# First SwiGLU of a hybrid DiT layer: input products as seven products of quarters, output sums accumulated in DRAM

## The chip, the cores and the metric

The kernel runs on one core of a Trainium2 chip. Its engines, each with its own instruction stream in order, are TensorE (PE; PEld is its loading of weights), VectorE (DVE), ScalarE (ACT), GpSimd (POOL) and SyncE (SP), which here only starts DMAs. DMAs go through 16 shared engines. The metric is device time in microseconds (us) of one execution.

## The reference

One layer of a diffusion transformer, batch 1, 512 latent tokens x (width 1024) and 256 context tokens ctx. What matters here is its first part, a modulated SwiGLU of width 2816 on both streams:

```python
def modulate(x, w, shift, scale):
    return rmsnorm(x, w) * (1 + scale) + shift

def swiglu(x, w_in, w_out):
    a, b = jnp.split(x @ w_in, 2, axis=-1)
    return (jax.nn.silu(a) * b) @ w_out
...
        h = h + 0.5 * g1 * swiglu(modulate(h, norm_ffn1[layer], sh1, sc1), w_ffn1_in[layer], w_ffn1_out[layer])
        hc = hc + 0.5 * g1c * swiglu(modulate(hc, norm_ffn1[layer], sh1c, sc1c), w_ffn1_in[layer], w_ffn1_out[layer])

        u = modulate(h, norm_mix[layer], sh2, sc2)
        uc = modulate(hc, norm_mix[layer], sh2c, sc2c)
...
        h = h + g2 * mixer_output(o, rg, cv, ga, gb, *branch_w)

        h = h + 0.5 * g3 * swiglu(modulate(h, norm_ffn2[layer], sh3, sc3), w_ffn2_in[layer], w_ffn2_out[layer])
    return rmsnorm(h, final_norm)
```

The shifts, scales and gates are nine vectors for each stream, c @ w_mod (1024 x 9216). Between the two SwiGLUs stand the retention, the convolution and their merge; the context ends with its keys and values.

## The kernel before

Channels lie on the 128 partitions, tokens in the free dimension, so an activation is eight blocks of 128 channels (`h0`..`h7` with 512 latent tokens, `hc` with 256 context tokens). Every product is in three matmuls (`mm3`, L90 to L92): each operand is split into a high part in fp32r and the low rest, and high x high, low x high and high x low are added up in PSUM. A weight unit (512 KB: `wraw`, four buffers) is loaded by SP, cast by ACT to `wh` (L81) and its rest taken by DVE as `wl` (L83). PSUM has eight banks of 512 columns (`ps`).

The first SwiGLU has 22 chunks of 128 hidden channels, each with two column blocks of w_in (the two halves a and b), in three groups of 8, 7 and 7 (`GROUPS`). A chunk multiplies both blocks with all eight channel blocks of the normed latent tokens (`uh`, `ul`: 48 matmuls of 512 columns) and of the context tokens (`uc`: 48 of 256). Then ACT takes the silu and DVE multiplies (L297, L304) and takes the low parts (L279). After a group, four out units multiply the group's chunks with w_out, two channel blocks each, and DVE adds the result, times the gate, to `h` and `hc` in SBUF (`residual`, L427). In the last group, the last two units come apart: four context products first, then the latent tokens by halves of 256, while ACT and DVE already sum the squares and norm the result for the next part (`tail1`, L252 to L271), and POOL saves h to `hdram`.

The first two chunks are computed in `start`, as the norms of the eight channel blocks come; the modulation vectors that these need are computed there by PE, DVE (L161) and POOL (L164) from loads of w_mod (`first_mods`). The 56 other modulation products (`mods`: one or two VectorE instructions of 1024 elements, L184) are spread beside the first SwiGLU by `mod_step`, two after each chunk and out unit. A scheduler sets each engine's order from the program and the tiles' waits; tiles of one tag share buffers, `t` has six.

## Time and profile before

Median of three runs 1779.48 us (1778.73 to 1779.65). The profiled execution has a span of 1775.7 us; some 3.8 us lie around the span.

| what | value |
|---|---|
| span of the profiled execution | 1775.7 us |
| time, median of 3 runs | 1779.48 us |
| ACT casts of weights, L81 | 248, 1.04 us each |
| DVE low parts of weights, L83 | 248, 1.21 us each |
| DVE residuals of the first SwiGLU, L427 | 68, 44.6 us |
| bytes moved by DMA | 199.95 MB, mean 113 GB/s |

A row of a timeline is start, duration, engine, line, operation and tiles; a group of equal rows has its count (x4). A matmul's duration includes its way through the array, so the price of one in a row is the distance between two starts.

### The profile page before, as it was taken

Reading aid. Unit: us, or ns where it says so; the run is one execution under the profiler, and the core shown is the slowest. Engines: PE = TensorE matmul, PEld = TensorE weight load, DVE = VectorE, ACT = ScalarE, POOL = GpSimd, SP = SyncE. Lnnn points to the kernel's source line nnn. Section 1 sums busy time; section 2 is a strip of 40 time slices with the busy share of each in tenths; the row PEclk is TensorE's granted clock in tenths of the full one; section 3 lists DMA queues with packets and bytes.
Section 4 is the critical chain, followed back from the end, with each engine's and each line's share of the span. In section 5 each row is a group of like instructions: output and inputs, shape, how many; then the busy total and the mean of one; then the engine's idle time right before and its main releaser. Section 6 shows DMA issues by size and latency. Waiting matters only on the chain. (4 is left out here: it accounts for less than half of the span.)

```text
span 1775.7 us, 22456 instructions
## 1 busy us (share of the span) xinstructions
PE 1749.0 (98%) x9182; PEld 1498.7 (84%) x9182; DVE 1038.7 (58%) x1646; ACT 575.1 (32%) x809; POOL 65.9 (4%) x111
## 2 busy tenths in 40 slices
PE   6999999999999999999999999999999999999997
PEld 4788888888889988888888888888888988888887
DVE  7755825452444798793876679293755643333335
ACT  5422113211222532432342334233562432222222
POOL 4100000000000000000000000001100000000000
PEclk8999999999999999999999999999999999999999
DMA  9133523362433321152142125114652133233321
GB/s 349 37 119 119 187 74 121 127 194 74 133 121 125 103 92 64 60 166 71 49 144 94 60 72 173 65 48 166 201 196 102 60 119 95 97 95 97 103 84 48
DMA packets 60156, 199.95 MB, mean 113 GB/s; under 512 B 7250, under 2 KB 7250, under 8 KB 60052
## 3 DMA queue, kind: packets, MB, share of 16 engines
q1 hardware_dynamic: 53140, 176.20, 29.8%
q0 software_dynamic: 6336, 21.25, 3.6%
q8 instruction: 72, 1.18, 0.3%
q10 hardware_dynamic: 576, 1.05, 0.2%
q14 instruction: 32, 0.26, 0.0%
HBM read 185.89 MB, written 12.58 MB: 112 GB/s over the span
## 5 line engine op out<-in xcount | busy, mean ns | idle before, releaser
L81 ACT CAST wh<-wraw 128x1024 fp32r<-128x1024 f32 (+1 forms) x248 | 257.2, 1038 | 640.3 <-PE ps L91 390.1
L83 DVE TENSOR_TENSOR wl<-wraw,wh 128x1024 fp32r<-128x1024 f32 (+1 forms) x248 | 298.5, 1206 | 255.9 <-ACT wh L81 251.7
L92 PE MATMUL ps<-uh,wl 128*128 128x512 f32 (+1 forms) x992 | 373.5, 377 | 2.2 <-DVE wl L83 2.2
L90 PE MATMUL ps<-uh,wh 128*128 128x512 f32 (+1 forms) x992 | 375.4, 380 | 0.3 <-ACT uh L270 0.3
L91 PE MATMUL ps<-ul,wh 128*128 128x512 f32 (+1 forms) x992 | 373.5, 377 | 0.0
L90 PE MATMUL ps<-gx,wh 128*128 128x512 f32 (+1 forms) x748 | 277.6, 373 | 0.2 <-ACT gx L278 0.2
L92 PE MATMUL ps<-gx,wl 128*128 128x512 f32 (+1 forms) x748 | 277.6, 372 | 0.0
L91 PE MATMUL ps<-gx,wh 128*128 128x512 f32 (+1 forms) x748 | 277.5, 372 | 0.0
L92 PEld LDWEIGHTS ps<-uh,wl 128*128 128x128 f32 x992 | 187.2, 189 | 37.2 <-DVE wl L83 2.9
L90 PEld LDWEIGHTS ps<-uh,wh 128*128 128x128 f32 x992 | 186.9, 189 | 34.7 <-issue 1.1
L91 PEld LDWEIGHTS ps<-ul,wh 128*128 128x128 f32 x992 | 187.3, 189 | 33.4 <-issue 0.5
L515 DVE SCALAR_TENSOR_TENSOR h<-y,vec,h 128x512 f32<-128x512 f32 x240 | 179.7, 749 | 5.4
L90 PEld LDWEIGHTS ps<-gx,wh 128*128 128x128 f32 x748 | 140.7, 188 | 24.6 <-ACT gx L278 0.4
L92 PEld LDWEIGHTS ps<-gx,wl 128*128 128x128 f32 x748 | 140.5, 188 | 24.6
L91 PEld LDWEIGHTS ps<-gx,wh 128*128 128x128 f32 x748 | 140.6, 188 | 24.0
L91 PE MATMUL ps<-uc,wh 128*128 128x256 f32 (+1 forms) x508 | 150.9, 298 | 0.2 <-DVE uc L271 0.2
L90 PE MATMUL ps<-uc,wh 128*128 128x256 f32 (+1 forms) x508 | 150.6, 297 | 0.3 <-ACT uc L270 0.3
L92 PE MATMUL ps<-uc,wl 128*128 128x256 f32 (+1 forms) x508 | 150.5, 297 | 0.0
L427 DVE SCALAR_TENSOR_TENSOR h<-ps,g_x,h 128x512 f32<-128x512 f32 (+1 forms) x68 | 44.6, 656 | 129.5 <-PE ps L92 129.2
L91 PE MATMUL ps<-gc,wh 128*128 128x256 f32 (+1 forms) x320 | 102.6, 321 | 0.0
L90 PE MATMUL ps<-gc,wh 128*128 128x256 f32 (+1 forms) x320 | 102.4, 320 | 0.0
L92 PE MATMUL ps<-gc,wl 128*128 128x256 f32 (+1 forms) x320 | 102.4, 320 | 0.0
(217 smaller groups left out, 2195.7 us busy)
## 6 DMA issues: line engine op xcount, KB each, us to landing
wraw<-in_w_mod SPq DMA_DIRECT2D x56, 512.0 KB, 3.5
wraw<-in_w1i SPq DMA_DIRECT2D x44, 512.0 KB, 3.8
wraw<-in_w2i SPq DMA_DIRECT2D x44, 512.0 KB, 3.7
wraw<-in_w_cv SPq DMA_DIRECT2D x16, 512.0 KB, 3.7
wraw<-in_w_v SPq DMA_DIRECT2D x16, 512.0 KB, 6.5
wraw<-in_w_rg SPq DMA_DIRECT2D x16, 512.0 KB, 3.6
wraw<-in_w_ro SPq DMA_DIRECT2D x16, 512.0 KB, 3.8
ypart<-t POOLq DMA_DIRECT2D x32, 256.0 KB, 4.3
```

The costliest lines, as they stand in the source:

```text
L81: nc.scalar.copy(hi, raw)
L83: nc.vector.tensor_sub(lo, raw, f32(hi))
L90: nc.tensor.matmul(o, w[0], x[0], start=first, stop=False)
L91: nc.tensor.matmul(o, w[0], x[1], start=False, stop=False)
L92: nc.tensor.matmul(o, w[1], x[0], start=False, stop=last)
L427: nc.vector.scalar_tensor_tensor(dst, p, g[:, b:b + 1], dst, ALU.mult, ALU.add)
L515: nc.vector.scalar_tensor_tensor(o, y[:, t:t + L], vec[:, w0 + t:w0 + t + 1], o, ALU.mult, ALU.add)
```

## The change

Four chunks stay as they are. For the other 18, the two column blocks of w_in and the tokens are taken as quarters: the contraction of 1024 channels in two halves of 512, the output as block a and block b, and the 768 tokens (latent and context side by side, tiles `uh`/`ul` now of 768) as two halves of 384. Strassen's scheme, in Winograd's form, replaces the eight products of quarters by seven, each with four channel blocks and three matmuls: 84 matmuls of 384 columns instead of 96. The sums of the tokens' quarters are made once (`operands`), those of the weights for every chunk, and the results are added up by VectorE and in PSUM (`chunk`).

```diff
+GROUPS1 = ((0, 4), (4, 4), (8, 4), (12, 4), (16, 3), (19, 3))
+LA = L + LC
+H = LA // 2
...
+    def operands(kb):
+        b1, b2 = hx[kb], hx[kb + 4]
+        b11, b12, b21, b22 = b1[:, :H], b1[:, H:], b2[:, :H], b2[:, H:]
+        ta, tb = t_((P, 2, H), F32, "wy", 2), t_((P, 2, H), F32, "wy", 2)
+        nc.vector.tensor_sub(ta[:, 0, :], b11, b12)
+        nc.vector.tensor_sub(ta[:, 1, :], b12, b22)
+        nc.vector.tensor_sub(tb[:, 0, :], ta[:, 1, :], b11)
+        nc.vector.tensor_add(tb[:, 1, :], b21, tb[:, 0, :])
...
+            split(hi, lo, t)
...
+    def chunk(j, u, t):
...
+        w0 = weights(r0)
+        nc.vector.tensor_add(y0[:, 0, :], a21, a11)
+        nc.vector.tensor_add(y0[:, 1, :], a21, a22)
+        w1 = weights(y0.rearrange("p a b -> p (a b)"))
+        nc.vector.tensor_add(y1[:, 0, :], y0[:, 1, :], a11)
+        nc.vector.tensor_add(y1[:, 1, :], y1[:, 0, :], a12)
+        w2 = weights(y1.rearrange("p a b -> p (a b)"))
+        w3 = weights(a22)
...
+        product(pa, w0, 0, part(u[:4], lo_), True)
+        nc.scalar.copy(p1, pa)
+        product(pd, w1, 0, [x[1] for x in t], True)
+        nc.scalar.copy(p7, pd)
+        product(pa, w0, 1, part(u[4:], lo_), False)
+        nc.scalar.activation(s[:, lo_], pa, AF.Silu)
+        product(pc, w1, 1, [x[0] for x in t], True)
+        nc.vector.tensor_sub(p7, p7, pc)
+        product(pb, w2, 0, [x[2] for x in t], True)
+        nc.vector.tensor_add(p1, p1, pb)
+        nc.vector.tensor_sub(c[:, hi_], p7, p1)
+        product(pc, w2, 1, part(u[4:], hi_), False)
+        nc.vector.tensor_add(s[:, hi_], p1, pc)
+        nc.scalar.activation(s[:, hi_], s[:, hi_], AF.Silu)
+        product(pd, w3, 0, [x[3] for x in t], False)
+        nc.vector.tensor_sub(c[:, lo_], pd, p1)
+        nc.vector.tensor_mul(s, s, c)
```

SBUF doesn't hold h beside the new operands. So h and hc live in DRAM during the first SwiGLU: two DRAM copies put x and ctx there at the start, each out unit of the first five groups sends its scaled result by accumulating DMAs, and the last group loads them again.

```diff
+        nc.gpsimd.dma_start(hdram, a["xT"])
+        nc.gpsimd.dma_start(hcdram, a["ctxT"])
...
+    def part_sum(b, px, pc):
+        r, rc = tmp(), tmp()[:, :LC]
+        nc.scalar.activation(r, px, AF.Identity, scale=hg["x1"][:, b:b + 1])
+        nc.gpsimd.dma_start(hdram[:, b, :], r, accum_op=ALU.add)
+        nc.scalar.activation(rc, pc, AF.Identity, scale=hg["c1"][:, b:b + 1])
+        nc.gpsimd.dma_start(hcdram[:, b, :], rc, accum_op=ALU.add)
+
+    def open_h():
+        pools.pop("left1").release()
+        open_pool("left2", "left")
...
+        for b in range(KT):
+            nc.sync.dma_start(h[b], hdram[:, b, :])
+        for i in range(4):
+            nc.sync.dma_start(hc2[i], hcdram[:, 2 * i:2 * i + 2, :])
```

Groups are (4, 4, 4, 4, 3, 3); the modulation products are spread as four steps beside each of chunks 2 and 3, one beside each Strassen chunk and two beside each out unit of the first five groups. The norm of `start` also writes the normed tokens in full fp32 (one more ACT pass for each block), for `operands`. The last unit of the last group has three chunks in place of seven under the latent halves. SBUF is reorganised in pools that follow each other; the raw tiles of `first_mods` have 16 buffers instead of 24, and later tiles (the merge's gates) take other places.

```diff
-    rtags = [f"gx{i}" for i in range(16)] + [f"gc{i}" for i in range(8)]
+    rtags = [f"{t}{i}" for i in range(8) for t in ("th", "tl")]
...
+            norm_start(b, xs, r1, deriv["x1"], *u[b])
...
+        nc.scalar.activation(src, v, AF.Identity, bias=sh)
...
+                if k0:
+                    keep(j, chunk(k0 + j, u, t))
+                    mod_step(1)
+                    continue
...
+                keep(j, plain(pa, pb, pc))
+                mod_step(4)
```

**How the order moves.** VectorE before, from the end of the context's norm through the low parts of the weights of chunk 2 (`wl_836`, `wl_842`) to those of chunk 3 (`wl_972`, `wl_978`):

```order
L83 TENSOR_TENSOR wl_836<-wraw_832,wh_834 128x1024
L83 TENSOR_TENSOR wl_842<-wraw_838,wh_840 128x1024
L304 TENSOR_TENSOR t_813<-t_813,ps_707 128x256
L297 TENSOR_TENSOR t_819<-t_819,ps_187 128x512
L279 TENSOR_TENSOR gc_190_816<-t_813,gc_190_816 128x256
L83 TENSOR_TENSOR wl_972<-wraw_968,wh_970 128x1024
L279 TENSOR_TENSOR gx_193_823<-t_819,gx_192_822 128x512
L304 TENSOR_TENSOR t_826<-t_826,ps_708 128x256
L83 TENSOR_TENSOR wl_978<-wraw_974,wh_976 128x1024
```

VectorE after the change, the last rows ahead of the low part of chunk 3's first weights (`wl_1045`); `wy`, `th` and `tl` are the operands' sums and their parts, `hx` the kept chunks' parts, L203 a modulation product:

```order
L368 TENSOR_TENSOR wy_876<-hx_8_81,wy_876 128x384
L298 TENSOR_TENSOR hx_203_894<-sg_828,hx_202_893 128x768
L203 SCALAR_TENSOR_TENSOR t_1025,mx<-wraw_1023,kh_84 128x1024
L298 TENSOR_TENSOR tl_199_886<-wy_876,th_198_885 128x768
L437 TENSOR_TENSOR sg_1008<-sg_1008,ps_911 128x256
L203 SCALAR_TENSOR_TENSOR t_1027,mc<-wraw_1023,kl_85 128x1024
L298 TENSOR_TENSOR hx_215_1014<-sg_1008,hx_214_1013 128x768
L203 SCALAR_TENSOR_TENSOR t_1031,mx<-wraw_1029,kh_84 128x1024
L203 SCALAR_TENSOR_TENSOR t_1033,mc<-wraw_1029,kl_85 128x1024
L203 SCALAR_TENSOR_TENSOR t_1037,mx<-wraw_1035,kh_84 128x1024
L203 SCALAR_TENSOR_TENSOR t_1039,mc<-wraw_1035,kl_85 128x1024
L101 TENSOR_TENSOR wl_1045<-wraw_1041,wh_1043 128x1024
```

Before, three small operations stood between the weights of chunk 2 and those of chunk 3; now all operands, three chunks' splits and eight modulation products stand ahead of the latter.

SyncE after the change, at the end of the first SwiGLU: the last loads of w_out, those of the next part's first weights, and behind them the loads of h:

```order
L97 DMA wraw_5318<-in_w1o 128x768
L97 DMA wraw_5624<-in_w_k 128x1024
L97 DMA wraw_5630<-in_w_k 128x1024
L97 DMA wraw_5719<-in_w_q 128x1024
L97 DMA wraw_5725<-in_w_q 128x1024
L610 DMA gx_980_5164<-hdram 128x512
L610 DMA gx_981_5165<-hdram 128x512
```

Before, no load of h stood there. And VectorE at the same place, from the last unit's weights (`wl_5322`) through the kept chunk to the residuals, which wait for these loads:

```order
L421 TENSOR_TENSOR sg_5060<-sg_5060,sg_5061 128x768
L101 TENSOR_TENSOR wl_5322<-wraw_5318,wh_5320 128x768
L298 TENSOR_TENSOR hx_979_5157<-sg_5060,hx_978_5156 128x768
L587 SCALAR_TENSOR_TENSOR gx_980_5164<-ps_5194,g_x_1185,gx_980_5164 128x512
L101 TENSOR_TENSOR wl_5628<-wraw_5624,wh_5626 128x1024
L587 SCALAR_TENSOR_TENSOR gx_981_5165<-ps_5195,g_x_1185,gx_981_5165 128x512
```

The residuals of the last group (L587, with `gx` and `gc` now the names of h and hc) stand behind every load that SyncE issues before them.

More of the change, by code (lines that the diff above doesn't have):

```diff
@@ L389, in start @@
                 products(1, b - 2)
-        sqc = [square_sum(accc, hc[j], j) for j in range(KT)][-1]
+        sqc = [square_sum(accc, hx[j][:, cx], j) for j in range(KT)][-1]
         products(0, 7)
@@ L459, in tail1 @@
         if n == 7:
-            st["u"] = u_tiles()
             norm_mods(h, st["ra"], deriv["x2"], st["u"], HALVES[0], range(4))
-    ffn(a["w1i"], a["w1o"], u, uc, [f"gx{i}" for i in range(16)], evac1, evac1c, mod_step, start, tail1)
+    h = ffn1(u_tiles())
+    pools.pop("right1").release()
+    open_pool("right2", "right")
     lg = cp.tile([P, 8], F32, name="lg")
```

223 lines of the change are left out of this document (159 added, 64 removed).

## The prediction

> **What bounds the kernel now.** I read the page first: busy times, then the forty slices.
>
> ```profile
> span 1775.7 us, 22456 instructions
> PE 1749.0 (98%) x9182; PEld 1498.7 (84%) x9182; DVE 1038.7 (58%) x1646; ACT 575.1 (32%) x809; POOL 65.9 (4%) x111
> PE   6999999999999999999999999999999999999997
> DVE  7755825452444798793876679293755643333335
> DMA  9133523362433321152142125114652133233321
> ```
>
> TensorE is busy 98% of the span, so time falls by what its matmuls shrink, less whatever waits the change brings it. VectorE is at 58% on average, but some slices stand at 9. So I read the stretches that the change touches: chunks 2 and 3 (80 to 120 us) and the end of the first SwiGLU (580 to 640 us).
>
> ```profile
> 80.00:100.00 20.00, 20.00 (x126) 18.11 (x126) 9.62 (x13) 7.49 (x12) 0.00 (x0) 1.00 0.32 107
> 100.00:120.00 20.00, 20.00 (x124) 17.98 (x123) 9.53 (x17) 4.38 (x7) 0.00 (x0) 1.00 0.31 106
> 600.00:620.00 20.00, 20.00 (x165) 19.78 (x165) 18.83 (x49) 16.50 (x26) 1.61 (x3) 1.00 0.50 159
> 620.00:640.00 20.00, 20.00 (x155) 19.39 (x154) 18.39 (x35) 9.69 (x16) 0.00 (x0) 1.00 0.21 73
> ```
>
> The columns after the sum are the busy times of PE, weight load, DVE, ACT and POOL, then granted clock, DMA share and GB/s. PE is full in all four. DVE is half empty at chunks 2 and 3, and at 94% and 92% where the SwiGLU ends: there it has no room, here it has 10 us in 20.
>
> **The change: the products.** What a matmul costs is its distance from the next one in the timeline.
>
> ```profile
> 399.72 0.39 PE L90 MATMUL ps<-gx,wh 128*128 128x512 f32 x1
> ...
> 401.08 0.39 PE L90 MATMUL ps<-gx,wh 128*128 128x512 f32 x1
> ```
>
> Six steps of 512 columns in 1.36 us: 0.227 us.
>
> ```profile
> 300.01 0.28 PE L90 MATMUL ps<-uc,wh 128*128 128x256 f32 x1
> ...
> 300.97 0.28 PE L92 MATMUL ps<-uc,wl 128*128 128x256 f32 x1
> ```
>
> Eight steps of 256 columns in 0.96 us: 0.120 us. A plain chunk is 48 x 0.2275 + 48 x 0.120 = 16.68 us. A Strassen chunk is 84 matmuls of 384 columns, a size that no row shows; between the two it would be 0.1738 us, 14.60 us a chunk. The bounds are 0.171 (512's price for each column) and 0.180 (256's), and far out 0.2275. I take the line between its two neighbours: 18 chunks save 18 x 2.08 = 37.4 us (28 to 42). In the last out section a block of three instead of seven chunks moves 48 pairs of 256-column halves back to 512: about 0.6 us. Gross: **-38 us** (-29 to -43).
>
> **VectorE's part of a Strassen chunk.** Steps of VectorE, start to start:
>
> ```profile
> 87.38 1.23 DVE L83 TENSOR_TENSOR wl<-wraw,wh 128x1024 fp32r<-128x1024 f32 x1 [1.14 <-ACT wh L81]
> 88.52 0.69 DVE L279 TENSOR_TENSOR gx<-t,gx 128x512 fp32r<-128x512 f32 x1
> 89.12 0.42 DVE L304 TENSOR_TENSOR t<-t,ps 128x256 f32<-128x256 f32 x1
> 99.11 1.22 DVE L184 SCALAR_TENSOR_TENSOR t<-wraw,kh 128x1024 bf16<-128x1024 f32 x1
> 100.26 0.08 DVE L184 DVE_READ_ACCUMULATOR t<-wraw,kh 128x1 f32 x1
> 603.36 1.65 DVE L269 SCALAR_TENSOR_TENSOR t<-o,ab_c,ps 128x256 f32<-128x256 f32 x4
> 604.93 1.67 DVE L271 SCALAR_TENSOR_TENSOR uc<-t,ab_c,uc 128x256 fp32r<-128x256 f32 x4
> ```
>
> So 1024 elements step in 1.14 us, 512 in 0.60, 256 in 0.34 (0.42 less the same overlap of 0.08; 0.39 with a scalar), a modulation product in 1.23; 384 and 768, between them, in 0.47 and 0.87. A chunk gives VectorE three wl of 1024, one of 512, four sums of 512, five of 384, two operations of 768 and, in group 1, two modulation products: 3.4 + 0.6 + 2.4 + 2.3 + 1.7 + 2.5 = 12.9 us beside 14.60 us of PE. It fits, with 1.7 us to spare, and better where a modulation is one product. I cost it at nothing; if that cover goes, each us over costs 18.
>
> **Four terms against it.** (1) The start: two DRAM copies, 3 MB, are issued on POOL right behind the load of rope, so at about 3.3 us, ahead of most loads.
>
> ```profile
> 2.70 0.56 POOL L402 DMA_DIRECT2D rope<-in_rope  x1
> 10.00:20.00 10.00, 8.93 (x38) 4.92 (x36) 6.70 (x18) 7.92 (x14) 2.35 (x2) 0.83 1.04 389
> 20.00:30.00 10.00, 6.36 (x39) 4.44 (x39) 10.00 (x19) 2.67 (x7) 5.32 (x4) 0.77 1.04 393
> 26.04 0.73 DVE L269 SCALAR_TENSOR_TENSOR t<-h,ab,ps 128x512 f32<-128x512 f32 x1
> ```
>
> The engines are full (share 1.04, about 390 GB/s) from 10 us on, so 3 MB cost 0 to 7.7 us, zero if what they push back is not yet wanted. VectorE is full from 20 us, with the first norm at 26.04; it starts on what has landed by then, and the copies take up to half of the rate until then: **+5**.
>
> (2) Chunk 3. In the new order VectorE has, between the end of the context's norm and the low part of chunk 3's first weights: 16 sums of 384 (7.5), 11 splits of 768 (9.6), 3 wl (3.4), 8 modulation products (9.8), two gatings of 512 (1.2) and three of 256 (1.0): 32.5 us, and about 1 us for steps that wait on the step before.
>
> ```profile
> 78.36 0.88 DVE L271 SCALAR_TENSOR_TENSOR uc<-t,ab,uc 128x256 fp32r<-128x256 f32 x2
> 85.95 0.40 PE L90 MATMUL ps<-uh,wh 128*128 128x512 f32 x1
> ```
>
> The norm ends at 79.2, 0.7 later with ScalarE's added pass: the weights come at 113.4. PE begins chunk 2 at 85.95, ends it at 102.6, and has six products of chunk 3 that need no low part (1.4 us): 104.8 with the same 0.7. PE waits **+9** (5 to 14: by the casts that the splits wait for). The next unit's weights stand ten operations behind, under chunk 3's 16.7 us.
>
> (3) The end. Let E be PE's end of the last chunk. The gating and the last out unit's wl end at about E+2.5. That wl frees the buffer for which SyncE's last w_q load waits, and the twelve loads of h and hc stand behind it.
>
> ```profile
> 3.31 3.25 SPq L360 DMA_DIRECT2D h<-in_xT  x7
> h<-hdram POOLq DMA_DIRECT2D x8, 256.0 KB, 4.6
> ```
>
> At 0.46 us an issue and 4.6 us to land, the first h is there at E+8.2, the first hc at about E+13. PE has gone through two units (6.26 us each) and four context products (4.3 us) by E+16.9; VectorE, who could begin late only, does its last context residual at about E+18.7. From there the chain is as before:
>
> ```profile
> 583.55 0.48 DVE L427 SCALAR_TENSOR_TENSOR o<-ps,g_c,o 128x256 f32<-128x256 f32 x1 [1.06 <-PE ps L92]
> 625.19 1.27 DVE L271 SCALAR_TENSOR_TENSOR ul<-t,ab_x,uh 128x256 fp32r<-128x256 f32 x3
> ```
>
> 22.6 us from 584.0 to the context's norm (606.6, the uc row above) and 42.5 to the latent one (626.5). Before, PE had 8 x 21 x 0.120 = 20.2 us of its own there; now 8 x 9 x 0.120 = 8.6. So it wants the context's norm at E+25.5 and gets it at E+41.3; half of the key products go ahead as blocks come, and with 2.9 us behind the last block it is at E+44.2 where without waits it were at E+31.3: 12.9 late. The latent norm adds up to 2.6. **+14**; 7 if the 6 us that VectorE itself waited for PE in this chain vanish, 20 if the loads land 5 us later.
>
> (4) The clock. Where PE has gaps at the start, it runs slower after them:
>
> ```profile
> 50.00:60.00 10.00, 7.98 (x37) 5.21 (x36) 9.17 (x18) 2.18 (x8) 6.16 (x4) 0.83 0.00 0
> 58.44 0.63 PE L90 MATMUL ps<-uh,wh 128*128 128x512 f32 x1
> 58.86 0.63 PE L91 MATMUL ps<-ul,wh 128*128 128x512 f32 x1
> ```
>
> 0.42 us instead of 0.227 at a granted clock of 0.83. For the new waits I take **+2** (0 to 5). The Trainium skill ("TensorE: Matmul & The Clock Gate", "What's actually happening") speaks against the change here: it has the array fall to half clock after an idle window of about 3.4 us and need about 3.4 us of work to come back. By that, an estimate from this page, each long wait costs 1.7 us more, with three waits about 5, and the sum below would be -5 in place of -8. The 0.42 us agrees with the half clock; how long it lasts after one wait no row shows.
>
> **What I cost at nothing.** Output sums: ScalarE's scaled copies and POOL's 80 accumulating transfers replace VectorE's residuals; PE needs only that banks come free, and each unit has 24 x (0.2275 + 0.120) = 8.34 us. 16 raw buffers for 24: the loads of four blocks still run ahead. The first SwiGLU's pools, and the gates' tiles later, change no work.
>
> **Sum:** -38 + 5 + 9 + 14 + 2 = **-8 us** on the profiled execution, whose 1775.7 us span lies 3.8 us under the median 1779.5 (what lies around it stays). So 1771.5 us.
>
> **Rivals.**
> - *B, the gain comes through*: the copies hide, and VectorE's waits are at their low ends: -38 + 0 + 5 + 7 + 0 = -26, 1753 us, down to 1741 with no wait at all. For it: VectorE's 10 free us in 20 at chunks 2 and 3. Against it: 33 us of work ahead of one weight.
> - *C, the accumulating transfers bind (slower)*. The tiles t have six buffers, and each out unit takes four of them until its transfers have landed, modulations and chunks the others. A landing of over 8.3 us makes ScalarE's next copy wait, over about 14 us (8.34 more, less the copies) PE's banks. Past 14 us each us costs 20 units x 1 us, so at 14.4 the gain is gone, and at 16 the time is 1779.5 - 8 + 40 = 1811. No row shows an accumulation; the nearest is
>
> ```profile
> ypart<-t POOLq DMA_DIRECT2D x32, 256.0 KB, 4.3
> ```
>
>   so it would have to be over three times as long. The Trainium skill ("Collectives: The Full Stack", "The bandwidth ceiling: the fold count and why AG ≠ RS ≠ AR") says that an adding transfer reads two sources and goes at half the rate; that would be 8.6 us here, an estimate, which fills the first slack but not the second. No trace here shows it.
> - *D, the change doesn't shorten the products*: 384 columns cost what 512 do. 84 x 0.2275 = 19.1 us, 18 x 2.4 = 44 us more in place of 37 less: 1779.5 + 44 + 30 = 1853. The rows of 256 speak against it.
> - *E, all waits at their upper ends*: -38 + 8 + 14 + 20 + 5 = +9: 1788 us.
>
> **How the numbers follow.** What one can tell from no change is 0.2%, 3.6 us. Forecast 0.54 (its own range, by the four terms, 1761 to 1784: faster 0.37, same 0.14, slower 0.03), B 0.20 (faster), C 0.12 (slower 0.10, same 0.02), D 0.03, E 0.11 (slower 0.08, same 0.03). Faster 0.57, same 0.19, slower 0.24. The range reaches from the middle of B to just past E: 1752 to 1790; outside lie half of B, D and most of C, 0.2 in all.
>
> **What would show it.** Matmuls at L400 stepping in 0.174 us (0.2275 is D). PE's largest waits at chunk 3's wl (L101), about 9 us, and at the residuals' squares and the norms after the last chunk, about 14 together. First norm about 5 us later than 26 us. Accumulating transfers landing under 8 us; ScalarE waiting for them at L598 is C. Waits of PE inside the Strassen chunks, on wl at L356, would make the forecast too low: I have none there.

## The result: slower, and the profile after

The changed kernel takes 1822.99 us (median of 4 runs, 1815.69 to 1826.29) against 1779.57 us before: a ratio of 1.024, 95% interval 1.0217 to 1.0263. The span grew by 44.2 us, where -8 was forecast. The page of the changed kernel, its span, busy times, three of the forty-slice rows and GpSimd's DMA queue:

```profile
span 1819.9 us, 22626 instructions
PE 1740.2 (96%) x8918; PEld 1506.7 (83%) x8918; DVE 1148.4 (63%) x1796; ACT 673.6 (37%) x963; POOL 138.3 (8%) x193
PE   5888999989899789999999999999999999999998
DVE  5895958566665678877579398474665643333335
DMA  9248475654764513133124115213562233233331
q0 software_dynamic: 17936, 40.13, 9.8%
```

TensorE has 264 matmuls fewer, and yet the first third of its row, nines before from the second slice on, has eights in it and a seven just behind; the DMA row stands at 4 to 8 in slices 3 to 13, where it was 2 to 6. The same queue line on the page before:

```profile
q0 software_dynamic: 6336, 21.25, 3.6%
```

(packets, MB, share of 16 engines' span.) Behind the first SwiGLU hardly anything differs. The same matmul, before and after:

```profile
648.53 0.28 PE L90 MATMUL ps<-gx,kh 128*128 128x256 f32 x1
```

```profile
692.90 0.28 PE L109 MATMUL ps<-gx,kh 128*128 128x256 f32 x1
```

It is 44.4 us late, so the whole difference lies ahead of this row. The products themselves are as cheap as forecast:

```profile
300.17 0.33 PE L400 MATMUL ps<-th,wh 128*128 128x384 f32 x1
...
302.94 0.33 PE L400 MATMUL ps<-tl,wh 128*128 128x384 f32 x1
```

Sixteen steps in 2.77 us: 0.173 us each, 14.55 us a chunk; four Strassen chunks without a wait are 58.3 us, and an out section of a group of four 33.7, of three 25.4 (144 matmuls).

**Where the time went.** From the start of each stage on TensorE, in the timelines (us; G1 to G4 the Strassen groups ahead of the last, O0 to O3 the out sections of the groups of four):

| stage | without waits | after | late |
|---|---|---|---|
| start of chunk 2 | 85.95 (before) | 93.70 | 7.75 |
| chunk 3 | 16.7 | 25.6 | 8.9 |
| O0, O1, O2, O3 | 33.7 each | 39.6, 38.1, 34.5, 34.2 | 12 |
| G1, G2, G3, G4 | 58.3 (G4 43.7) | 64.1, 60.0, 67.2, 51.0 | 24 |
| the end, to 692.90 (the rest of the 44.4) | | | 31 |

So some 83 us stand against a gain of 38 to 39. The end's 31 is a remainder, but it comes out directly as well: the next part's first products start 45.05 us after the last chunk, where the prediction has 25.5 without waits, and from there to the row at 692.90 it takes 54.2 us, before 42.2; that is 19.5 and 12.0. The 36 us in O and G are those that the prediction costed at nothing. Some 10 of the 12 lie in O0 and O1, where a modulation product is two VectorE instructions (all of them in O0, half in O1); in O2 and O3 it is one. Only one execution of each kernel is profiled, and those of the changed kernel lie between 1815.69 and 1826.29 us, so a few us between the stages of two kernels can be chance.

*Chunk 3* takes as long as forecast. TensorE waits 6.76 us and then works at a lower clock (the last row's duration, 0.63 for 0.40; the granted clock is 0.50 from 114.4 to 121.2):

```profile
110.59 0.40 PE L109 MATMUL ps<-ul,wh 128*128 128x512 f32 x1
117.75 0.80 PE L108 MATMUL ps<-uh,wh 128*128 128x512 f32 x1 [6.76 <-ACT wh L99]
118.34 0.63 PE L109 MATMUL ps<-ul,wh 128*128 128x512 f32 x1
```

The wait ends with ScalarE's cast of the chunk's second weights, and that cast waits for their load. SyncE issues the chunk's two loads with 8 us between them, because the second needs a raw buffer, which VectorE's modulation products hold until they are done:

```profile
104.81 8.39 SPq L97 DMA_DIRECT2D wraw<-in_w1i  x2
116.65 1.04 ACT L99 CAST wh<-wraw 128x1024 fp32r<-128x1024 f32 x1 [4.08 <-DMA wraw<-in_w1i]
```

The low parts that the prediction had in mind (L101) follow at 118.22, just behind.

*An out section and the group behind it.* Windows of the changed kernel over O2 and the start of G3 (busy PE, weight load, DVE, ACT, POOL; granted clock; DMA share; GB/s):

```profile
349.00:359.00 10.00, 10.00 (x63) 8.86 (x62) 3.52 (x5) 4.03 (x7) 4.25 (x6) 1.00 1.07 204
359.00:369.00 10.00, 10.00 (x57) 8.58 (x56) 3.51 (x5) 3.78 (x6) 4.65 (x6) 1.00 1.08 255
369.00:379.00 10.00, 7.75 (x41) 6.07 (x40) 6.87 (x10) 5.00 (x7) 1.72 (x2) 1.00 0.87 192
379.00:389.00 10.00, 6.75 (x39) 6.43 (x38) 5.81 (x9) 1.92 (x3) 0.00 (x0) 0.92 0.71 220
```

The DMA engines are full at 204 to 255 GB/s, where the start of the kernel before moved 390 at the same share. TensorE is full while the sums go out; it waits in the next group. The timelines of SP's queue, VectorE and TensorE there:

```profile
355.49 7.23 SPq L197 DMA_DIRECT2D wraw<-in_w_mod  x2
363.53 0.33 SPq L380 DMA_DIRECT2D wraw<-in_w1i  x1
...
376.00 0.33 SPq L197 DMA_DIRECT2D wraw<-in_w_mod  x1
...
378.26 0.33 SPq L381 DMA_DIRECT2D wraw<-in_w1i  x1
```

```profile
386.44 0.69 DVE L386 TENSOR_TENSOR wy<-wraw,wraw 128x512 f32<-128x512 f32 x1 [4.19 <-DMA wraw<-in_w1i]
387.05 1.22 DVE L356 TENSOR_TENSOR wl<-wraw,wh 128x1024 fp32r<-128x1024 f32 x1
388.19 0.55 DVE L412 TENSOR_TENSOR t<-t,ps 128x384 f32<-128x384 f32 x1
```

```profile
388.79 0.69 PE L400 MATMUL ps<-uh,wh 128*128 128x384 f32 x1 [3.25 <-DVE t L412]
```

Read upwards: TensorE waits for a subtraction of the chunk in work (L412), which frees its bank. That stands in VectorE's queue behind the sums of the next chunk's weights (L386), and those weights have just landed: their load was issued at 378.26, behind a load of modulation weights at 376.00, and took 8.2 us (the median of w1i is 5.7, before 3.8). The first chunk's load, at 363.53, stands behind two more, which took 7.2 us to get their raw buffers. In O0 and O1 the modulation products wait in their turn for scratch (`t`, six buffers) that output sums hold until their transfers land, and so does ScalarE; two rows of O1:

```profile
252.07 1.23 DVE L203 SCALAR_TENSOR_TENSOR t<-wraw,kl 128x1024 bf16<-128x1024 f32 x1 [5.40 <-DMA hdram<-t]
264.49 0.47 ACT L600 ACTIVATE t<-ps,g_c 128x256 f32<-128x256 f32 x1 [4.34 <-DMA hdram<-t]
```

*The end.* The last chunk ends at 593.61 (E). VectorE's first residual, its first context residual and steps of the norms, TensorE's three longest waits, and windows at half clock:

```profile
601.12 0.75 DVE L587 SCALAR_TENSOR_TENSOR gx<-ps,g_x,gx 128x512 f32<-128x512 f32 x1 [3.83 <-DMA gx<-hdram]
608.82 0.88 DVE L587 SCALAR_TENSOR_TENSOR gc<-ps,g_c,gc 128x256 f32<-128x256 f32 x2 [2.66 <-DMA gc<-hcdram]
641.62 0.48 DVE L290 SCALAR_TENSOR_TENSOR ul<-t,ab_c,uh 128x256 fp32r<-128x256 f32 x1
659.76 1.26 DVE L288 SCALAR_TENSOR_TENSOR t<-gx,ab_x,ps 128x256 f32<-128x256 f32 x3 [8.19 <-PE ps L266]
665.54 0.89 DVE L290 SCALAR_TENSOR_TENSOR ul<-t,ab_x,uh 128x256 fp32r<-128x256 f32 x2 [0.19 <-ACT uh L289]
```

```profile
615.57 0.38 PE L108 MATMUL ps<-hx,wh 128*128 128x256 f32 x1 [3.79 <-DVE gx L587]
638.00 1.22 PE L266 MATMUL ps<-t,ones 128*128 128x256 f32 x2 [4.56 <-DVE t L259]
678.18 0.80 PE L108 MATMUL ps<-gx,kh 128*128 128x256 f32 x2 [4.48 <-ACT gx L297]
```

```profile
630.00:635.00 5.00, 3.44 (x15) 3.15 (x15) 2.79 (x6) 2.54 (x3) 2.15 (x4) 0.50 0.23 79
635.00:640.00 5.00, 2.00 (x7) 1.83 (x8) 4.96 (x16) 1.63 (x5) 0.00 (x0) 0.50 0.74 225
```

The first load of h comes when forecast (E+7.5 for E+8.2), the first of hc some 2 us later than forecast (E+15.2 for E+13). The chain behind them is slower: context normed at E+48.5 instead of E+41.3, the latent tokens at E+72.8 instead of E+61.2. On the context's way TensorE's pieces run at half clock (a granted clock of 0.50 from 616.15 to 622.98 and from 629.80 to 643.45). On the latent tokens' way it is TensorE's order: VectorE has its part ready at 646.8 and then waits 8.19 us for a matmul (L266, at 659.12) that stands behind 144 products of the next part since the one at 638.00, most of them at a granted clock of 1.00; before, 96 such products stood between the same two. After these products TensorE has little left to do and waits 4.48 us at 678.18 for the next part's own chain; before, its wait there was 0.52 us.

### The profile page after: what moved, and what is told of

Read it like the earlier page. It is cut to its first block, busy times and chain, and to the rows that moved or that the text cites. A ratio compares the mean times of both kernels' runs of the same rounds, so it can differ in the third digit from the quotient of the medians.

```text
span 1819.9 us, 22626 instructions
## 1 busy us (share of the span) xinstructions
PE 1740.2 (96%) x8918; PEld 1506.7 (83%) x8918; DVE 1148.4 (63%) x1796; ACT 673.6 (37%) x963; POOL 138.3 (8%) x193
## 4 chain that ended last, share of the span: by engine, by line
PE 74%; issue 11%; DVE 6%; DMA 6%; POOL 1%; ACT 1%; DVEq 0%; SPq 0%; POOLq 0%; ACTq 0%
PE ps L108 21%; PE ps L109 21%; PE ps L110 21%; PE ps L400 10%; DMA wraw<-in_w1i 2%; DMA wraw<-in_w1o 1%; DVE wl L101 1%; DMA hx<-in_xT 1%; DVE t L203 1%; DMA wraw<-in_dist_x 1%; DVE h L697 1%; DMA th<-in_w_mod 1%; POOL t L183 1%; POOL hcdram L601 0%; ACT wh L99 0%
## 5 line engine op out<-in xcount | busy, mean ns | idle before, releaser
L99 ACT CAST wh<-wraw 128x1024 fp32r<-128x1024 f32 (+2 forms) x212 | 219.4, 1036 | 557.5 <-PE ps L109 303.9
L101 DVE TENSOR_TENSOR wl<-wraw,wh 128x1024 fp32r<-128x1024 f32 (+2 forms) x212 | 254.3, 1202 | 243.3 <-ACT wh L99 238.2
L109 PE MATMUL ps<-ul,wh 128*128 128x512 f32 (+1 forms) x832 | 299.1, 361 | 0.1
L109 PE MATMUL ps<-gx,wh 128*128 128x512 f32 (+1 forms) x544 | 204.0, 377 | 0.0
L108 PE MATMUL ps<-gx,wh 128*128 128x512 f32 (+1 forms) x544 | 203.7, 377 | 0.2 <-ACT gx L297 0.2
L108 PE MATMUL ps<-hx,wh 128*128 128x512 f32 (+1 forms) x364 | 124.2, 341 | 10.4 <-DVE gx L587 6.0
L110 PE MATMUL ps<-hx,wl 128*128 128x512 f32 (+1 forms) x364 | 123.6, 340 | 1.1 <-DVE wl L101 1.1
L109 PE MATMUL ps<-hx,wh 128*128 128x512 f32 (+1 forms) x364 | 123.4, 339 | 0.0
L108 PEld LDWEIGHTS ps<-gx,wh 128*128 128x128 f32 x544 | 102.1, 188 | 18.9 <-ACT gx L297 0.4
L109 PEld LDWEIGHTS ps<-gx,wh 128*128 128x128 f32 x544 | 102.0, 188 | 18.7
L400 PE MATMUL ps<-th,wh 128*128 128x384 f32 x288 | 97.5, 339 | 4.0 <-ACT wh L355 3.9
L400 PE MATMUL ps<-tl,wh 128*128 128x384 f32 x288 | 96.5, 335 | 0.0
L400 PE MATMUL ps<-th,wl 128*128 128x384 f32 x288 | 95.8, 335 | 0.0
L108 PEld LDWEIGHTS ps<-hx,wh 128*128 128x128 f32 x364 | 70.6, 194 | 18.9 <-DVE gx L587 6.5
```

The source lines that it names most:

```text
L99: nc.scalar.copy(hi, raw)
L101: nc.vector.tensor_sub(lo, raw, f32(hi))
L108: nc.tensor.matmul(o, w[0], x[0], start=first, stop=False)
L109: nc.tensor.matmul(o, w[0], x[1], start=False, stop=False)
L110: nc.tensor.matmul(o, w[1], x[0], start=False, stop=last)
L400: nc.tensor.matmul(o, w[i][:, ws], x[k][m], start=first and k == n == 0, stop=k == 3 and n == 2, skip_group_check=True)
```

## Experiments

Theory at the outset: the adding transfers fill the DMA engines, so that weights come late (T). Rival: VectorE's own load in the Strassen chunks, with modulation products between, does it, and the transfers only go along (R). All times are medians beside runs of the kernel before on the same chip. Lateness is against the stages without waits in the table above.

### 1. Output sums written plainly

```diff
-        nc.gpsimd.dma_start(hdram[:, b, :], r, accum_op=ALU.add)
+        nc.gpsimd.dma_start(hdram[:, b, :], r)
```

(and the same for `hcdram`.)

> The changed kernel with one thing altered: the 80 transfers of the output sums write to DRAM without adding, so the sums of the first five groups are left out. Theory T (the DMA engines are full in the out units because an adding transfer costs more than twice a plain one, weights then land late, and PE waits in out group 0 and in the first Strassen chunks of a group): of the 35.5 us that the groups and out units lose, at least 25 go, time 1823 - 25 = 1798 or less, and the DMA share in the out units falls from 0.98 to about 0.7. Rival R (the loss is VectorE's own order and length in a Strassen chunk, whatever the transfers do): within 5 us of the changed kernel, 1818 to 1826.

Measured 1801.87 us (1.0129, 1.0114 to 1.0144), 21 us less. Its page and, over O2, its windows:

```profile
q0 software_dynamic: 11536, 40.13, 6.3%
hdram<-t POOLq DMA_DIRECT2D x40, 256.0 KB, 3.6
```

```profile
341.00:351.00 10.00, 10.00 (x59) 8.68 (x58) 3.52 (x5) 3.61 (x6) 2.26 (x5) 1.00 0.58 201
351.00:361.00 10.00, 10.00 (x61) 8.77 (x60) 3.51 (x5) 4.20 (x7) 2.71 (x5) 1.00 0.76 278
```

The out sections are late by 2 us instead of 12 (34.5, 34.1, 33.7, 34.2), the Strassen groups by 16 instead of 24 (64.9, 60.8, 61.8, 47.5). The same bytes take 6.3% of the engines' time instead of 9.8%, and the loads of w1i land after 5.0 us instead of 5.7. So about half of the 36 us goes with the adding, where T had asked for 25 us and R for none: neither expectation was met.

### 2. Plain chunks, all else as changed

```diff
-                if k0:
-                    keep(j, chunk(k0 + j, u, t))
-                    mod_step(1)
-                    continue
-                wa, wb = units(a["w1i"][j])
+                wa, wb = units(a["w1i"][k0 + j])
```

> The changed kernel with plain chunks in place of the 18 Strassen chunks; copies, accumulating transfers, groups, operands and the spread of the modulations stay. PE has 37.6 us more to do. Theory T (the waits come from late weights, which plain chunks need as well): most of the 35.5 us in groups and out units stay, and the time is 1845 to 1860. Rival R (the waits come from the Strassen chunk's own VectorE work): they go, and the time is 1820 to 1832, so that Strassen's scheme gains next to nothing by itself.

Measured 1841.06 us (1.0348, 1.033 to 1.0366): between the two. The seven products gain 18 us of the 37 worked out. A group of four plain chunks is 66.65 us without waits; the groups took 67.6, 66.6, 67.6 and 52.5 (for 50.0): 4 us late, where Strassen groups are 24. The 20 us between are the other half of Strassen's gain: a plain chunk hides what stands beside it, a Strassen chunk does not. Two things differ, and this run does not separate them: the plain chunk is 2.1 us longer, and it has no subtraction on VectorE (L412) that TensorE needs and that stands behind the next chunk's sums.

### 3. The start and chunk 3: copies later, modulation products later

Copies behind a small write of the first norms' scales, so that they run from about 65 us:

```diff
+        for d, x in ((hdram, a["xT"]), (hcdram, a["ctxT"])):
+            nc.gpsimd.dma_start(d[:, 0, 0:32], ab1.rearrange("p a b c -> p (a b c)"))
+            nc.gpsimd.dma_start(d, x)
...
-        nc.gpsimd.dma_start(hdram, a["xT"])
-        nc.gpsimd.dma_start(hcdram, a["ctxT"])
```

> The changed kernel with the two DRAM copies of x and ctx put behind a small write that waits for the last of the first modulations (about 65 us), where the trace shows the DMA engines idle. Theory T (the copies take the rate from the first loads): chunk 2 begins at about 86.5 us in place of 93.7, time 7 us less, 1816. Rival (the start is longer for the 16 raw buffers or ScalarE's added pass): chunk 2 begins after 91 us and the time falls by under 3 us.

The eight modulation products after chunks 2 and 3, not between them:

```diff
-                mod_step(4)
+            if k0 == 0:
+                mod_step(8)
```

> The changed kernel with the eight modulation steps of chunks 2 and 3 put behind both chunks in the program, so that VectorE has chunk 3's weights ahead of them. Theory T (chunk 3 waits for the modulation products ahead of its weights): PE's 6.8 us wait there falls under 2 us, and chunk 3 takes 17 to 18 us in place of 25.6; time down 6 to 9, 1815. Rival (the work is only pushed on: out group 0's weights now stand behind the products): chunk 3 gains as much, out group 0 loses it, time within 3 us of 1823.

And both together:

> Two earlier edits together: the copies behind the small write (16 us less by itself) and the modulations of chunks 2 and 3 behind both chunks (9 less). If the two causes are separate, the gains add up: 1823 - 25 = 1798. If both only shift the same wait (chunk 3's, or out group 0's), it stays above 1803.

Measured 1806.94 (1.0158, 1.0142 to 1.0173), 1814.16 (1.0203, 1.0186 to 1.022) and 1805.57 us (1.0151, 1.013 to 1.0172). With the copies held, chunk 2 starts at 82.54: they cost 11.2 us of the start, over the upper bound of 7.7 (9.5 and 9.1 by two later kernels with the copies held, at 84.22 and 84.56). Without them the start is 1.4 to 3.4 us shorter than before, so neither the fewer raw buffers nor ScalarE's added pass lengthens it. The time fell by 16 us, more than the start gained; in this execution O and G are 29 us late instead of 36, for which there is no reason on record. With the products after, chunk 3 takes 17.0 us: the whole 8.9 goes, and O0 takes 43.4 us. Together the edits don't add up: chunk 3 gains as much, but O0 takes 45.0 us for 38.7 with the copies alone, since the eight products now stand in it.

### 4. The place of the modulation products

Early within each out section (3, 3, 2, 0 over its four units instead of 2 each), with adding and then with plain transfers:

```diff
-                    mod_step(2)
+                    mod_step((3, 3, 2, 0)[mm])
```

> The changed kernel with the eight modulation steps of an out group spread as 3, 3, 2, 0 over its four out units instead of 2, 2, 2, 2. Theory P (see the run with five buffers): no modulation's load stands in front of a Strassen group's first weights, which are issued some 8 us earlier, and the groups' starts lose 2 to 4 us less each, time 1808 to 1816. Theory T (the full DMA engines in the out units are what matters): bytes and transfers are the same, so out group 0 and 1 keep their 6 and 5 us, and the time is within 4 us of 1823. Rival: with six products on VectorE the out units' own weights come late, and the time rises by some us.

> Plain writes of the output sums (sums of the first five groups left out) and the eight modulation products of each output group over its first three units (3, 3, 2, 0), so that none of their loads stands ahead of the next group's first weights. Plain writes alone: 1801.9, five Strassen groups late by 19 us. The early products alone, with adding transfers: groups late by 7 us instead of 24, but output groups later by 6 to 8 us each, 1831. Theory M (modulation loads ahead of the first weights make the rest of the groups' loss; the output groups lost only because the DMA engines were full): groups late by under 8 us, output groups by under 3 us each, 1788 to 1794. Rival (three products between two units are too many for the load buffers whatever the transfers do): output groups late by over 5 us each, 1802 or more.

Measured 1831.06 (1.0295, 1.0279 to 1.0311) and 1807.30 us (1.0161, 1.0146 to 1.0176). With adding transfers the groups are 7 us late instead of 24, but the out sections 38 instead of 12. The second one's Strassen groups take 60.0, 58.4, 58.2 and 43.7 us: 2 us late in all. Its windows in the second of them:

```profile
299.00:309.00 10.00, 10.00 (x60) 10.00 (x59) 7.54 (x12) 3.39 (x5) 0.00 (x0) 1.00 0.34 117
309.00:319.00 10.00, 10.00 (x59) 10.00 (x58) 9.93 (x14) 5.05 (x8) 0.00 (x0) 1.00 0.43 131
```

TensorE is full beside Strassen chunks in which VectorE is at up to 99%: the chunk's own chain holds, one modulation product a chunk included. But O0 to O3 take 41.8, 38.4, 36.2 and 36.1 us, 18 late, against 2 with two products a unit. The groups are as the theory had them, the time is the rival's, and of the rival's sign (over 5 us in each out section) only O0 shows it. What is late is the weights of the unit or chunk behind a run of modulation loads; moving the loads moves the wait. Its queue and its waits in O1:

```profile
240.02 11.70 SPq L197 DMA_DIRECT2D wraw<-in_w_mod  x3
253.68 0.33 SPq L97 DMA_DIRECT2D wraw<-in_w1o  x1
```

```profile
250.13 1.23 DVE L203 SCALAR_TENSOR_TENSOR t<-wraw,kl 128x1024 bf16<-128x1024 f32 x1 [3.31 <-DMA hdram<-t]
```

```profile
259.43 0.50 PE L108 MATMUL ps<-hx,wh 128*128 128x512 f32 x1 [3.01 <-ACT wh L99]
```

Three loads take 11.7 us to issue. Each waits for a raw buffer, that is, for VectorE to do an earlier product; one of these waits 3.31 us for scratch that an output transfer holds. The w_out load stands behind them.

Spread thin instead (section 3's two edits, one a unit, two a chunk from the third group on):

> The kernel before this one in this set, with one modulation step beside each out unit instead of two, and two beside each Strassen chunk from the third group on. Theory T (in an out group the DMA engines have 6 MB of plain loads, some 15 us at 390 GB/s, and 3 MB of adding transfers, some 21 us at 147 GB/s, for 33.6 us of PE): 2 MB less is 5 us less, so out groups no longer fill the engines; the out groups fall to 34 us each and the Strassen groups start with less delay: 8 to 15 us less, 1783 to 1790. Rival (the chunks' own chain, or VectorE with one more product in a chunk): within 4 us of 1798.

Measured 1796.95 us (1.0098, 1.008 to 1.0116). That is 8.6 us less than the run before it, as theory T had it; but that run had come out at 1805.57 and not at 1798, so the time lies above T's range and in the rival's. With one product a unit O1 to O3 take 33.7 us each, without a wait, although the transfers add (DMA share 0.76 in O1): so the adding alone does not delay a unit. The Strassen groups are no better: they are 24 us late in all, 11 of it in the last one (54.6 us instead of 43.7), which was free before.

### 5. More buffers

A fifth raw buffer, paid for with one buffer of the silu's scratch; then that scratch alone as control:

```diff
-        return t_(shape, F32, "wraw", 4)
+        return t_(shape, F32, "wraw", 5)
...
-        s, c = t_((P, LA), F32, "sg", 3), t_((P, LA), F32, "sg", 3)
+        s, c = t_((P, LA), F32, "sg", 2), t_((P, LA), F32, "sg", 2)
```

> The changed kernel with five buffers of raw weights (wraw) instead of four, room for which comes from two instead of three buffers of the gated products (sg). Theory P (what the plain writes left of the loss, 19 us in the Strassen groups, comes from the ring of four buffers: the modulation's loads hold two of them until VectorE has used them, so a group's first pair of weights is issued too late): the Strassen groups lose 5 to 10 us less, time 1813 to 1818, and the first chunk's cast no longer waits for a DMA. Rival (it is the length of the chain from raw weights over sums, casts and low parts in a chunk, whenever the loads come): within 3 us of 1823.

> The changed kernel with two buffers instead of three for the activation's scratch and nothing else: the room that the ring runs take is taken from there. Both theories: within 2 us of the changed kernel's 1823 us. If it is over 1826, the scratch buffers themselves are a part of what the run with a fifth weight buffer lost.

Measured 1829.48 (1.0287, 1.0268 to 1.0305) and 1817.10 us (1.0223, 1.0196 to 1.0249): with the fifth buffer the kernel is 12 us slower than with the scratch alone, and outside both expectations. Its out sections take 33.9, 39.1, 33.7 and 33.7 us, 6 late instead of 12, but its groups 65.1, 67.4, 70.0 and 55.0, 39 late instead of 24: the wait has moved, and why the sum grew is open. The control is 6 us under the changed kernel, where 2 were expected, but its executions (1814.84 to 1823.79) and the changed kernel's lie over each other. So the scratch isn't the reason. Then a buffer of its own for the modulation weights, with adding and plain transfers (sums left out as in 1; the silu's scratch as in the control):

```diff
-        raw = raw_tile((P, D))
+        raw = t_((P, D), F32, "mraw", 1)
```

> The modulation weights get a load buffer of their own (one), so that the ring of four belongs to the block weights alone; scratch as in the run beside it. Theory P (the Strassen groups lose their 24 us because a modulation product queued on VectorE holds a buffer that a Strassen weight load needs): the five groups lose under 12 us, time 1806 to 1814. Rival Q (the loads come late because the DMA engines are full and the one queue on SyncE is in order, so whose buffer it is does not matter; with one buffer the second of two modulation loads now holds that queue until VectorE has done the first product): 1820 to 1830.

> As the run before this, and the output sums written without adding (sums of the first five groups left out), so that the DMA engines have room. Measured with plain writes and the shared ring: 1801.9, with 19 us still lost in the Strassen groups. Theory P: the own ring takes at least 8 of these 19, time 1786 to 1794. Rival Q: within 4 us of 1802. Rival S (what is left is the order on VectorE: the next chunk's sums wait for their weights in front of the sums that TensorE wants): also within 4 us of 1802, but with waits on VectorE's sums whose weights land late in the trace.

Measured 1841.68 (1.0353, 1.0334 to 1.0372) and 1820.62 us (1.0241, 1.0215 to 1.0267): 19 us worse than the changed kernel and the run of section 1, outside every expectation. SP's queue, VectorE and TensorE in the first of them:

```profile
193.14 17.94 SPq L197 DMA_DIRECT2D mraw<-in_w_mod  x4
```

```profile
202.20 1.23 DVE L203 SCALAR_TENSOR_TENSOR t<-mraw,kh 128x1024 bf16<-128x1024 f32 x1 [3.45 <-DMA mraw<-in_w_mod]
204.50 0.55 DVE L412 TENSOR_TENSOR t<-t,ps 128x384 f32<-128x384 f32 x1
205.10 0.69 PE L400 MATMUL ps<-uh,wh 128*128 128x384 f32 x1 [10.19 <-DVE t L412]
```

With one buffer, the modulation loads come one at a time, and four of them hold SyncE's queue for 17.9 us. TensorE's wait of 10.2 us has another reason: the subtraction that it needs (L412) stands on VectorE behind three modulation products, each of which waits over 3 us for its load. So this edit puts a new wait into VectorE's queue, and it decides neither for the shared ring nor for the shared SyncE queue.

### 6. The end

All context products of the last group first, with hc loaded first:

```diff
+                w = [x for mm in range(4) for x in out_units(mm)]
+                pc = [ps((P, 2, LC)) for _ in range(4)]
+                for b in range(KT):
+                    proj(pc[b // 2][:, b % 2, :], w[b], gc_)
+                    evac1c(hc, b, pc[b // 2][:, b % 2, :])
...
-        for b in range(KT):
-            nc.sync.dma_start(h[b], hdram[:, b, :])
```

> The changed kernel with the last group's out units in another order: hc is loaded before h, and the context products of all eight blocks come first, then the latent blocks 0 to 3, then the halves. The same products; PE has 16.8 us of its own work behind the context's residuals instead of 8.6. Theory C (PE waits for VectorE's chain behind the last context residual): from the end of the last chunk to the first key products 45 us become 35 to 40, time 1813 to 1818. Rival (the loads' landing sets the stretch, whatever stands behind it): 44 us or more, time within 3 us of 1823.

A last group of four instead of three chunks (more of TensorE's work under the norms), and the loads of h and hc on ScalarE's queue:

```diff
-GROUPS1 = ((0, 4), (4, 4), (8, 4), (12, 4), (16, 3), (19, 3))
+GROUPS1 = ((0, 4), (4, 4), (8, 3), (11, 3), (14, 4), (18, 4))
```

> The changed kernel with groups (4, 4, 3, 3, 4, 4) instead of (4, 4, 4, 4, 3, 3): the last group has four chunks, the same chunks and products in all. Theory C (the last stretch costs what VectorE's chain of residuals, squares and norms lasts beyond PE's own work there): PE has 8.5 us more of its own work in the last out units, so from the end of the last chunk to the first key products 45 us stay 45 to 48 while 8.5 us more are done in them: time 1814 to 1818. Rival (the last stretch costs what the loads of h take, and everything behind follows by PE's own time): the stretch grows by 8.5 us, and the time is within 2 us of 1823.

```diff
-            nc.sync.dma_start(h[b], hdram[:, b, :])
+            nc.scalar.dma_start(h[b], hdram[:, b, :])
```

(and the same for hc.)

> The changed kernel with the twelve loads of h and hc issued on ScalarE's queue, not behind SyncE's loads of w_k and w_q. The first lands at E+7.5 us and the last near E+17 in the changed kernel (E: PE's end of the last chunk). Theory C: the loads may come 3 us earlier, and the last stretch falls by 0 to 4 us, 1819 to 1823, since VectorE's chain behind the context's last residual is what lasts. Rival (the loads' place behind SyncE's waits is the main cause): they come 4 us earlier or more and the stretch falls by as much and the clock's part besides, 1812 to 1816. ScalarE spends some time on twelve issues, which could cost a us or two.

Measured 1815.12 (1.0204, 1.0186 to 1.0222), 1822.76 (1.0257, 1.0235 to 1.0278) and 1823.19 us (1.0254, 1.0235 to 1.0272). From the last chunk to the next part's first product the changed kernel takes 45.05 us, these three 40.5, 45.5 and 45.1. In the first, half a us misses theory C's range for the stretch; the time is in its range, helped by out sections and groups that are 30 us late in this execution instead of 36. In the second, 8.5 us more of TensorE's work fit into the stretch at no cost: the chain through residuals and norms sets it, not TensorE. But the groups of three in the middle give it back: their out sections take 33.9 and 34.4 us for 25.4, their chunks 46.3 and 47.8 for 43.7. In the third, the issues took 11.3 us of ScalarE's queue; the first h was there at E+6.1 instead of E+7.5, the first hc at E+16.2 instead of E+15.2. So the loads as a whole came no earlier, and the run can't say what earlier loads would bring.

### 7. Together

No copies: the first group writes its sums plainly, and x and ctx are added from DRAM later (with the products spread as in 4):

```diff
+                        for d, x in ((hdram, a["xT"]), (hcdram, a["ctxT"])):
+                            nc.gpsimd.dma_start(d[:, :, 0:4], z, accum_op=ALU.add)
+                            for b in range(KT):
+                                nc.gpsimd.dma_start(d[:, b, :], x[:, b, :], accum_op=ALU.add)
```

> No DRAM copies at all: the first group's output sums are written plainly, and x and ctx are added from DRAM by adding transfers that a small write holds until the second group's first chunk. Modulations of chunks 2 and 3 behind both chunks, and spread as in the run before it. Theory T: out group 0 has 13 us less of DMA work and takes 34 us, while the second group's chunks have 20 us more and room for it (their share is about 0.4): 2 to 5 us less than the spread kernel, 1780 to 1787. Rival: the 3 MB of adding transfers stand on GpSimd's queue and in the DMA engines when the second group's out units come, and the time is the spread kernel's or more.

The spread kernel of 4 with the end of 6; and the same with the last products moved away from the last groups:

```diff
-                mod_step(1)
+                mod_step({8: 2 - mm % 2, 12: 2, 16: 0}.get(k0, 1))
```

> All edits that helped together: copies behind a small write, modulation products of chunks 2 and 3 after both, one per output unit and one or two per chunk, context products first in the last group. Measured apart: 1797.0 without the last, and the last took 4.5 us from the tail of the changed kernel (1815.1 against the run before it of 1822.8, with the gain of its tail measured at 4.5 us). If the two add: 1789 to 1793. Rival: the last group is late anyway by its own chunks (9 to 11 us lost there with products in them), so that the tail's gain is hidden: 1795 to 1800. No theory has it below the kernel before (1779.5).

> As the run with all helpful edits (1794.3), with the modulation products of the last output group before the end and of the last group's first chunk (4 and 2) moved into the third and fourth output groups, which were free of waits there. In that run TensorE waited 5.05 us in the last group's first chunks for VectorE's sums whose weights landed late, with the DMA engines full, and the group took 54.0 us instead of 43.7. Theory (the modulation loads beside the adding transfers make it): last group 44 to 46 us, third and fourth output groups still under 36 us, 1784 to 1788. Rival (the third and fourth output groups and the chunks behind them lose what the last gains): 1791 to 1796. Either way still slower than the kernel before.

Measured 1806.61 (1.0167, 1.0143 to 1.019), 1794.33 (1.009, 1.0068 to 1.0112) and 1796.02 us (1.01, 1.0084 to 1.0115). The first can't be held against its edit. In its profiled execution (1803.13 us) the first SwiGLU ends 5.7 us earlier than in the spread kernel, though O0 still takes 39.1 us and not 34; 12 us are lost behind it, where the code does not differ, 8 of them in the second SwiGLU from about 1440 us on, at steps of 512 columns of 0.233 us instead of 0.227 with TensorE full and a granted clock of 1.00. Why is open. The second, between its two expectations, is the best version, still 0.9% slower than the kernel before. TensorE in its last group:

```profile
524.48 0.34 PE L400 MATMUL ps<-th,wl 128*128 128x384 f32 x1
529.88 0.69 PE L400 MATMUL ps<-uh,wh 128*128 128x384 f32 x1 [5.05 <-DVE t L412]
```

In the third this group is free of waits (43.7 us), but G3, behind the out section with the added products, takes 71.0 us instead of 61.2, and G4 49.5 instead of 46.6: the rival's case. From O0 on, G and O (with the last group) are late by 36 us in the changed kernel, 28 in the second run of this section, 34 in the third, and 18 and 19 in the two with plain writes and the shared raw buffers: no placement tried brings it near nothing.

## Why the prediction was wrong

By its own steps:

- **Gross, -38: right.** 0.173 us a step for 0.1738, and groups without a wait take 14.6 us a chunk.
- **The start, +5: low.** 7.75 us at chunk 2, and 9 to 11 by the runs without the copies there; the upper bound was 7.7. The first norm came at 36.6 us instead of 26.0, not about 5 later.
- **Chunk 3, +9: right in size (8.9) and place, partly by luck.** The wait is 6.76 us; most of the rest is the lower clock behind it, which the prediction had as a term of its own. The modulation products are the cause, since the run with them behind both chunks has none of it. But they delay the chunk not only by standing ahead of its low parts on VectorE: they hold the raw buffer that a load of its weights needs, a link that the prediction did not have and that comes back below.
- **The clock, +2, and the end, +14: both mis-sized.** The end lost 31 us: 19.5 ahead of the next part's first products, where 12.9 were forecast, and 12.0 behind them, where up to 2.6 were. VectorE reached its last context residual at E+21.5 instead of E+18.7; from there the prediction carried over the chain of before, 22.6 us to the context's norm, where it took 27.0, and 42.5 to the latent one, where it took 51.3. Before, TensorE was full in that stretch. Now its granted clock was 0.50 for 20.5 of the 27.3 us from 616.15 to 643.45, so its part of the context's chain is slower as well; and the latent chain waited 8.19 us for TensorE's order, which the prediction didn't look at. What each is worth was not tried. The clock was priced once, at 2 us, for three waits; the changed kernel's mean granted clock is 0.979 for 0.994. The Trainium skill ("TensorE: Matmul & The Clock Gate", "What's actually happening") was weighed for this; by the prediction's estimate from it a long wait costs 1.7 us more. The trace agrees in the 0.50, and behind the wait at chunk 3 it lasted 3.5 us of work (117.75 to 121.22), as the page has it; but the clock stood at 0.50 behind waits of 2.26 us (at 629.87) and 3.25 us (at 388.79) too, shorter than the page's idle window of some 3.4.
- **"What I cost at nothing": this is the step that failed.** It made two claims, that VectorE's 12.9 us fit beside 14.60 us of a chunk, and that TensorE needs of the output sums only that banks come free. Each was checked against its own engine. VectorE's sum does fit (the run with plain, early products: Strassen groups 2 us late in all). What was left out is what the two share: SyncE's one queue in order, four raw buffers and six scratch buffers. An output sum holds scratch until its transfer lands, a modulation product waits for scratch and holds a raw buffer, its successors' loads hold the queue, and a unit's or chunk's weights stand behind them. In a Strassen chunk this reaches TensorE through VectorE's order: a subtraction whose bank TensorE needs stands behind the sums of weights that have not landed. The prediction's sign, waits on the low parts at L356, was smaller (0.64 us at most); the waits that counted were on L412 (3.25 us there). Plain chunks of 16.7 us stood it (4 us late), Strassen chunks of 14.6 us don't (24 late), and out sections with two products and adding transfers in 8.3 us a unit don't either (12 late). That is 36 of the some 52 us missed; the end and its clock are 15, the start 3.
- **Rival C** named the adding transfers and the scratch, but set the point where it decides at a landing of 14 us. The median landing was 6.1 us, under the 8 us that "What would show it" asked for, and yet without the adding the kernel is 21 us faster: with the engines full, the loads of w1i and w_mod land after 5.7 and 4.2 us (median) instead of 5.0 and 3.6, and VectorE and ScalarE wait for scratch in the first out sections. The adding needs the products to do harm there: with one a unit, TensorE has no wait in O1 to O3.

Shown by runs: the copies' cost, chunk 3, the adding's 21 us, Strassen's net 18 us, that the remaining lateness moves with the modulation products' loads, and that the end is set by its chain and not by TensorE's own work. Argued from waits, not shown: that the shared queue, raw buffers and scratch are the whole of the remaining lateness. No run leaves the modulation products out, gives the output sums scratch of their own, or puts the modulation loads on another engine's queue, and the runs with more buffers (section 5) came out slower. Edits did not add up (section 3), so the shares that runs gave back one at a time overlap.

## What to carry to other kernels

A change that shortens an engine's work by an eighth takes as much cover from everything that was hidden under it: list what shares a queue or a buffer ring with the shortened stage, and price each against the shorter cover, not against its own engine's free time. Do the same for results that the engine now needs back from another engine, such as the subtractions here: they wait for all that stands ahead of them there. Work that is free anywhere in a slack schedule (here the modulation products, whose loads stand in order with the weights) has a price that moves with it once the slack is gone. A chain copied from an old profile holds only as long as the engines in it keep their clock and their order.

## What the runs showed of the hardware

An adding transfer from SBUF to DRAM is far dearer than a plain one. From the two q0 lines, 9.8% of 1819.9 us against 6.3% of the plain run's 1801.2 us: 65 us more of all 16 engines for 15.7 MB of sums. Written plainly, the 18.9 MB more than before (copies and sums) took 6.3% of the plain run's span less 3.6% of the span before, 50 us, some 380 GB/s. If copies and sums go at one rate, the sums take 41 us plainly and 106 us adding, about 148 GB/s, 0.39 of the rate (an estimate). The Trainium skill ("Collectives: The Full Stack", "The bandwidth ceiling: the fold count and why AG ≠ RS ≠ AR") has a step that adds, and so reads two sources, go at half the rate of a copy; here it is less, by this estimate. The median landing shows it only in part, 6.1 us for 3.6; the share of the engines shows it. GpSimd's issue takes longer as well; its groups from 130 to 560 us (count, busy, mean ns), adding and plain:

```profile
L599 POOL DMA_DIRECT2D hdram<-t x40 | 38.2, 954 | 389.1 <-ACT t L598 388.9
```

```profile
L599 POOL DMA_DIRECT2D hdram<-t x40 | 21.8, 544 | 395.0 <-ACT t L598 394.9
```
